# The first pair of a feed-forward as seven products instead of eight, and a new head of fourteen products

## The chip, the cores and the metric

The kernel runs on one core of a Trainium2 chip. The metric is the device time of one launch in microseconds (us). The kernel before takes 919.77 us, the median of three runs (919.72 to 920.04).

A core has five engines that run side by side, each with a queue that it works through in order: TensorE (PE) multiplies matrices from SBUF into PSUM, VectorE (DVE) and ScalarE (ACT) work element by element and may read and write both memories, GpSimd (POOL) does the same in SBUF alone, and SyncE (SP) issues DMA transfers. An instruction that waits for a semaphore holds up all that stands behind it on its own engine.

## The reference, cut to what matters

```python
x = x + 0.5 * rms_norm(swiglu_ffn(rms_norm(x, norm_pre[l, 0]), ffn1_w_in[l], ffn1_w_out[l]), norm_post[l, 0])
mixed = token_mixer(rms_norm(x, norm_pre[l, 1]), ...)
x = x + rms_norm(mixed, norm_post[l, 1])
x = x + 0.5 * rms_norm(swiglu_ffn(rms_norm(x, norm_pre[l, 2]), ffn2_w_in[l], ffn2_w_out[l]), norm_post[l, 2])

def swiglu_ffn(x, w_in, w_out):
    gate, up = jnp.split(x @ w_in, 2, axis=-1)
    return (jax.nn.silu(gate) * up) @ w_out
```

There are 512 tokens of width 1024, a feed-forward width of 2816, all in float32, and one layer. Each of the two feed-forwards computes gate and up (two products of 512 by 1024 with 1024 by 2816), a product of the two, and a last product back to width 1024. The change touches the first feed-forward's gate and up alone.

## The kernel before, in words

**Precision.** Each float32 operand is split in two fp32r parts, a high part (a copy that rounds) and a low part (what the copy left out). One product takes three matrix passes: high by high, high by low, low by high. For a weight tile the high part is an ACT cast of 128x1024 (line 294) and the low part a DVE subtraction of the same size (line 296), both in `split`.

**Pairs and products.** The 22 columns of 128 of gate and up are taken in 11 pairs, 0 to 10. Of a pair, gate and up and the two halves of the 1024 rows give four weight tiles of 512 KB: a (gate, upper rows), b (up, upper rows), c (gate, lower rows), d (up, lower rows). The tokens come in two halves of 256. Done plainly, a pair takes eight products of a weight tile with a block of the activations; `ffn_in` does a pair with seven, in the manner of Strassen and Winograd, from sums of weight tiles (line 310) and sums of activation blocks (`sums`, line 391). The products of a pair are called p1 to p7. p1 and p2 use the plain tiles a and c with the plain blocks of the first token half; p3 uses the plain tile d, and the four others use sums of weight tiles, or sums of activations, or both. A product (`prod`, line 604) is 24 matmuls of 128x256: 16 that read the weight tile's high part, then 8 that read its low part.

**The start.** The kernel begins with the first feed-forward, and there the sums of activations are not ready. So `HEADS` does pair 0 of the first feed-forward plainly, with eight products: c1 to c4 for the first token half, and e1 to e4 for the second, which use the same four weight tiles again (`held` keeps them in SBUF). Between these stand p1 and p2 of the pairs 1 and 2. That makes twelve products. While they run, `start` (line 736) writes out by hand in what order ACT, DVE and PE are given the rest: the norm of the token rows 2 and 3 (`norm`), their transposes, and the sums of activations, in five steps for each of the two rows (`to_s` begins a row's generator, and each `step(g2)` or `step(g3)` takes one step more). Every piece of work is issued where it stands in this text, and each engine's queue holds it in that order.

**The weight buffer.** The split weight tiles lie in one SBUF tile `w` with four places. `lie` (line 259) takes the first free place in the order of `free`; a place is given back when the product that reads it is issued (`drop`); and where no place at all is held, `split` sets the order anew: `if not self.slot and it.key[0] != "mix": self.free = deque(FREE2 if it.key[0] == "f2" else FREE)`, with `FREE = (2, 3, 0, 1)`. `full_split` splits one tile; `feed` splits tiles until four places are held. The first tiles go to three places of their own (`stay`), so three of pair 0's four tiles lie in these, and the fourth lies in place 2 of `w` from c2 until e2.

**Loads.** Weight tiles are loaded by SP into two rings, three buffers `raw` and five `raw2`, and a load waits until its buffer's last reader is done. The loads of the start are issued from the first us on, with those of x between them.

**The sums of weight tiles.** At the start POOL makes eight of them (pairs 1 and 2, four each; line 310, `late` is false); later DVE makes them. Each sum overwrites a raw tile, so it waits until that tile's last split is done, and the next split of the sum waits for POOL.

**After the head.** `ffn_in` runs the rest of `ORDER`, four tiles ahead (`feed`). For the pairs before `FILLED` the parts of a pair are added with DVE in SBUF; from there on more is gathered in PSUM. The second feed-forward has had its own head, `HEADS2`: p1 and p2 of seven pairs, fourteen products in all, none of which needs a sum of any kind; the tiles of the five pairs in `ONCE` are loaded for that alone and once more later.

## Time and profile before

| | |
|---|---|
| time, median of 3 runs | 919.77 us |
| time of the profiled execution | 920.66 us |
| its span (first to last instruction) | 918.9 us |
| mean granted TensorE clock over the span | 0.998 |
| DVE busy, ACT busy, POOL busy | 84%, 57%, 21% of the span |
| weight tiles of the two feed-forwards' first matrices loaded | 98, of 512 KB |

The profiled execution's time is 1.8 us over its span, for what lies around the first and last instruction. The rows that follow give for a group of instructions the line, the engine, the operation, what it writes and reads, the shape and type, the number of them, then the busy time and the mean in ns of one. A row of the timeline gives the start and the length of a run of like instructions in us, and in brackets the idle time of the engine before it and what ended that. The matmuls of one run overlap: one lasts 277 ns from its issue to its end, but they are issued every 114 to 118 ns.

### The profile page before, as it was taken

How to read it: one execution, taken by the hardware profiler on the slowest of the kernel's cores; microseconds unless marked ns; L12 is line 12 of the kernel's file. 1: busy time of each engine (PE TensorE's matmuls, PEld its weight loads, DVE VectorE, ACT ScalarE, POOL GpSimd, SP SyncE). 2: the span in 40 equal slices, each digit the busy share in tenths (PEclk: the TensorE clock that was granted, in tenths of full speed). 3: DMA queues.
4: the chain of work that ended last, by engine and by line, in shares of the span. 5: the costliest groups of instructions: out<-in, count | busy, mean ns of one | idle time of the engine just before them, and what ended most of it. 6: DMA issues, size and time to landing. Idle time of an engine off the chain costs nothing.

```text
span 918.9 us, 18150 instructions
## 1 busy us (share of the span) xinstructions
PE 910.2 (99%) x7332; PEld 877.3 (95%) x7332; DVE 768.1 (84%) x1007; ACT 524.2 (57%) x753; POOL 190.6 (21%) x267
## 2 busy tenths in 40 slices
PE   9999999999999999999999999999999999999997
PEld 8999999999999999998888887899999999999997
DVE  6899988889888877799877655699899989998886
ACT  7645555547666467957634345594454545757661
POOL 2531112121111047842330310313000000010002
PEclk9999999999999999999999999999999999999999
DMA  9355879775897825699852125252354445378542
GB/s 308 84 168 131 188 186 213 188 160 139 217 286 233 247 57 140 136 204 231 186 93 79 37 92 176 81 180 74 111 161 139 138 118 160 96 229 256 170 145 93
DMA packets 123384, 145.42 MB, mean 158 GB/s; under 512 B 12066, under 2 KB 96034, under 8 KB 123300
## 3 DMA queue, kind: packets, MB, share of 16 engines
q1 hardware_dynamic: 107332, 129.05, 46.3%
q0 software_dynamic: 15680, 14.69, 11.9%
q8 instruction: 57, 0.93, 0.4%
q10 hardware_dynamic: 288, 0.52, 0.2%
q14 instruction: 27, 0.22, 0.1%
HBM read 142.14 MB, written 31.46 MB: 189 GB/s over the span
## 4 chain that ended last, share of the span: by engine, by line
PE 57%; DVE 3%; ACT 2%; DMA 1%; issue 1%; SPq 0%; DVEq 0%; POOLq 0%; POOL 0%; ACTq 0%
PE ps L619 23%; PE ps L1012 8%; PE ps L549 5%; PE ps L1004 4%; PE ps L198 4%; PE ps L200 4%; PE ps L199 4%; PE ps L560 1%; PE ps L364 1%; DMA f2sums<-in_ffn_w_out_dram 1%; PE ps L1756 0%; PE ps L1451 0%; PE ps L1729 0%; DVE w L296 0%; DVE sT L1457 0%
## 5 line engine op out<-in xcount | busy, mean ns | idle before, releaser
L294 ACT CAST w<-raw 128x1024 fp32r<-128x1024 f32 x246 | 251.0, 1027 | 189.3 <-PE ps L619 89.4
L296 DVE TENSOR_TENSOR w<-raw,w 128x1024 fp32r<-128x1024 f32 x246 | 299.8, 1222 | 30.2 <-ACT w L294 28.8
L619 PE MATMUL ps<-xq,w 128*128 128x256 f32 x2016 | 237.4, 277 | 0.0
L619 PEld LDWEIGHTS ps<-xq,w 128*128 128x128 f32 x2016 | 233.2, 188 | 0.1
L619 PE MATMUL ps<-sq,w 128*128 128x256 f32 x1512 | 178.2, 277 | 0.0
L619 PEld LDWEIGHTS ps<-sq,w 128*128 128x128 f32 x1512 | 174.8, 188 | 0.0
L310 DVE TENSOR_TENSOR raw<-raw,raw 128x1024 f32<-128x1024 f32 x72 | 89.7, 1251 | 6.3 <-DMA raw<-in_ffn_w_in_dram 4.9
L1012 PE MATMUL ps<-w,hs 128*128 128x256 f32 x672 | 80.9, 276 | 0.0
L1004 PE MATMUL ps<-w,hs 128*128 128x256 f32 x672 | 79.2, 276 | 0.0
L1012 PEld LDWEIGHTS ps<-w,hs 128*128 128x128 f32 x672 | 78.3, 188 | 0.0
L1004 PEld LDWEIGHTS ps<-w,hs 128*128 128x128 f32 x672 | 77.5, 188 | 0.0
L198 PE MATMUL ps<-w,xq 128*128 128x512 f32 x176 | 71.6, 408 | 0.2 <-DVE sT L1457 0.2
L199 PE MATMUL ps<-w,xq 128*128 128x512 f32 x176 | 68.6, 391 | 0.0
L200 PE MATMUL ps<-w,xq 128*128 128x512 f32 x176 | 68.6, 391 | 0.0
L944 POOL DMA_DIRECT2D f2sums<-in_ffn_w_out_dram x15 | 20.1, 1484 | 175.2 <-DMA f2sums<-in_ffn_w_out_dram 174.9
L549 PE MATMUL ps<-xq,w 128*128 128x256 f32 x480 | 55.7, 277 | 0.0
L549 PEld LDWEIGHTS ps<-xq,w 128*128 128x128 f32 x480 | 54.9, 188 | 0.5 <-issue 0.5
L884 ACT CAST hs<-hf 128x1024 fp32r<-128x1024 f32 x32 | 33.7, 1053 | 28.0 <-PE ps L1012 20.3
L885 DVE TENSOR_TENSOR hs<-hf,hs 128x1024 fp32r<-128x1024 f32 x32 | 39.1, 1222 | 9.0 <-ACT hs L884 8.4
L944 POOL DMA_DIRECT2D f1sums<-f1sums x26 | 21.5, 828 | 110.0 <-DMA f1sums<-in_ffn_w_out_dram 57.9
L944 POOL DMA_DIRECT2D f2sums<-f2sums x30 | 26.1, 897 | 84.0 <-DMA f2sums<-in_ffn_w_out_dram 40.2
L310 POOL TENSOR_TENSOR raw<-raw,raw 128x1024 f32<-128x1024 f32 x12 | 32.6, 2721 | 40.9 <-DVE w L296 40.7
(279 smaller groups left out, 1248.0 us busy)
## 6 DMA issues: line engine op xcount, KB each, us to landing
raw<-in_ffn_w_in_dram SPq DMA_DIRECT2D x98, 512.0 KB, 4.7
raw<-in_ffn_w_out_dram SPq DMA_DIRECT2D x44, 512.0 KB, 4.9
raw<-in_w_mix_in_dram SPq DMA_DIRECT2D x28, 512.0 KB, 4.7
raw<-f2sums SPq DMA_DIRECT2D x15, 512.0 KB, 4.6
raw<-f1sums SPq DMA_DIRECT2D x13, 512.0 KB, 6.2
raw<-in_w_mix_out_dram SPq DMA_DIRECT2D x8, 512.0 KB, 3.9
f2sums<-in_ffn_w_out_dram SPq DMA_DIRECT2D x30, 128.0 KB, 6.0
f2sums<-in_ffn_w_out_dram SPq DMA_DIRECT2D x15, 256.0 KB, 6.0
```

The lines of the kernel that those rows point to most:

```text
L198: mm(ps, sh, mh, start=start, stop=False, **kw)
L199: mm(ps, sh, ml, start=False, stop=False, **kw)
L200: mm(ps, sl, mh, start=False, stop=stop, **kw)
L294: nc.scalar.copy(hi, raw)
L296: self.low = nc.vector.tensor_tensor(lo, raw, hi.bitcast(F32), op=ALU.subtract)
L310: added = (nc.vector if late else nc.gpsimd).tensor_tensor(o, o, c, op=ALU.add)
L549: mm(ps[:, u0:u1], w[:, a, k, :], self.xop(k, b, u0, u1), start=k + n + m == 0, stop=k == ND - 1 and n == 2, skip_group_check=True,)
L619: self.nc.tensor.matmul(ps[:, c], wb[b][:, k, v], left[d][:, k, :], start=first and a + n + k == 0, stop=n == 2 and k == KH - 1, skip_grou ...
L885: self.nc.vector.tensor_tensor(lo, src, hi.bitcast(F32), op=ALU.subtract)
L944: nc.gpsimd.dma_start(to[:, a:b], v, accum_op=ALU.add)
L1004: mm(out, a[kk][:, i * P : (i + 1) * P], w[:, b, kk, QUARTER * v : QUARTER * (v + 1)], start=begin and c == kk == n == 0, stop=kk == 1 and ...
L1012: mm(ps[:, QUARTER * c : QUARTER * (c + 1)], A[a][:, c], B[b], start=begin and c == n == 0, stop=n == 2, skip_group_check=True,)
```

## The change

The first feed-forward now does what the second did. Pair 0 is one more pair of seven products; the plain products c1 to e4 are gone, with the places that held their tiles. `HEADS` and `ORDER` are what `HEADS2` and `ORDER2` were, for both feed-forwards: the head is fourteen products, p1 and p2 of the pairs 3, 5, 7, 8, 6, 1 and 0, of which ten tiles (pairs 3, 5, 7, 8, 6) are loaded again later. The pairs follow as 0, 1, 2, 3, 4, 5, 9, 6, 7, 8, 10, `FILLED` is 2 for both, and POOL makes the eight sums of pairs 0 and 1. `start` is rewritten for the new head: p1's result is copied to SBUF with ACT before p2 adds to the same bank (line 616 of the change), and the places of the steps of the sums of activations are others. One product of 24 matmuls falls away.

The core of the diff:

```diff
-HEADS = [("c1", 0), ("c3", 0), ("c2", 0), ("c4", 0), ("p1", 1), ("e1", 0), ("e3", 0)]
-HEADS += [("e2", 0), ("p1", 2), ("p2", 1), ("e4", 0), ("p2", 2)]
...
-HEADS2, ORDER2 = (
+POOLED = {"f1": 2, "f2": 1}
+FILLED, ONCE, GATED = 2, (3, 5, 7, 8, 6), (1, 9, 6, 7)
 SEQ = (0, 1, 2, 3, 4, 5, 9, 6, 7, 8, 10)
+HEADS, ORDER = (
     [("p" + c[0], int(c[1])) for c in cs.split()]
     for cs in ("13 15 17 23 25 18 27 28 16 11 26 10 21 20", "50 51 60 61 70 30 40 71 31 12")
 )
...
+        alone = (7, 8) if name == "f2" else range(len(once))
+        own = {pt: [load(pt[1], place[pt[0]], None if n in alone else name, n)] for n, pt in enumerate(once)}
...
-                        nc.scalar.activation(L.col(), L.nhalf[:, :1], AF.Exp)
+                        nc.scalar.activation(L.col(), L.nhalf[:, :1], AF.Silu)
```

and in `start`, behind the first splits, as it now reads:

```python
        head, done = deque(HEADS), deque()

        def prod():
            self.lag()
            p, t = head.popleft()
            self.prod(p, t, False)
            done.append(lambda: self.after(p, t))

        after = lambda: done.popleft()()
        prod()
        root(2)
        self.full_split()
        prod()
        after()
        for h in range(2):
            nc.scalar.copy(gpre[:, v[h]], gain[h])
        self.full_split()
        norm(2)
        prod()
        step(q[0][1], q[1][1])
        step(q[0][1], q[1][1])
        self.full_split()
        step(q[0][0])
        after()
        self.to_s(2, xn[2])
        prod()
        root(3)
        after()
        self.full_split()
        norm(3)
        step(q[0][1], q[1][0], q[1][1])
        prod()
        after()
        self.full_split()
        self.to_s(3, xn[3])
        g2, g3 = self.gs
        prod()
        after()
        self.full_split()
        step(g2)
        prod()
        after()
        self.full_split()
        step(g3)
        for g in (g2, g3, g2, g3, g2, g3):
            prod()
            after()
            self.feed()
            step(g)
```

The head's products are called H1 to H14 below, in the order of `HEADS`: H1 to H3 are p1 of the pairs 3, 5, 7; H4 and H5 p2 of 3 and 5; H6 p1 of 8; H7 and H8 p2 of 7 and 8; H9 p1 of 6; H10 p1 of 1; H11 p2 of 6; H12 p1 of 0; H13 and H14 p2 of 1 and 0. In the rows, `raw_125`, `raw_30_210` and `raw_35_245` are the loaded tiles of H7, H8 and H9, `raw_37_278`, `raw_279` and `raw_398` those of H10, H11 and H12, and `raw_53_475` that of H13; `ps_320`, `ps_325` and `ps_400`, `ps_405` are the PSUM banks of the token rows 2 and 3, in which their sums are made; `sq_116` and `xq_76` are two of the blocks of activation sums. A semaphore's name tells which engine or queue is waited for.

**First place: the middle of the head.** ACT's queue in the kernel before, from the first tile of pair 2 (its p1, the ninth product) on:

```order
L294 CAST w<-raw_212 128x1024 [waits DMAHW2_49]
L398 CAST sq_116<-ps_336 128x4x128 [waits DVE_49,PE_49,Activation_49]
L646 COPY hf_113<-ps_386 128x2x256
L398 CAST sq_116<-ps_376 128x4x128 [waits DVE_49,PE_49]
L294 CAST w<-raw_11_124 128x1024 [waits DMAHW1_49]
L398 CAST xq_76<-ps_331 128x4x128 [waits DVE_49,PE_49,Activation_49]
L294 CAST w<-raw_212 128x1024 [waits PE_49,Pool_49]
```

and in the change, from the cast of H7's tile on:

```order
L278 CAST w<-raw_125 128x1024 [waits DMAHW0_49,DVE_49,PE_49]
L382 CAST sq_116<-ps_325 128x4x128 [waits DVE_49]
L616 COPY hf_113<-ps_413 128x2x256 [waits PE_49]
L278 CAST w<-raw_30_210 128x1024 [waits DMAHW1_49,PE_49,Activation_49]
L382 CAST sq_116<-ps_405 128x4x128 [waits DVE_49]
L618 ACTIVATE hf_113<-ps_285 128x2x256 [waits PE_49]
L278 CAST w<-raw_35_245 128x1024 [waits DMAHW2_49,PE_49,Activation_49]
```

Before, the casts of plain tiles (the first and the fifth row; the last is of a sum) wait for their load alone, since the places that they write are free. In the change each cast waits for PE as well (`PE_49`: the sixteenth matmul of the product before, the last that reads the high part of the same place), and between two of them stand a cast of a sum of activations, which waits for DVE, and a copy or Silu of a product's result.

DVE's queue at the same place, in the kernel before:

```order
L296 TENSOR_TENSOR w<-raw_212,w 128x1024 [waits DMAHW2_49,Activation_49]
L638 TENSOR_TENSOR hf_113<-ps_249,hf_113 128x2x256
L397 TENSOR_TENSOR ps_331<-ps_336,hf_113 128x512 [waits DVE_49]
L397 TENSOR_TENSOR ps_336<-ps_336,hf_113 128x512
L397 TENSOR_TENSOR sq_116<-ps_336,sq_116 128x4x128 [waits PE_49,Activation_49]
L397 TENSOR_TENSOR ps_371<-ps_376,hf_113 128x512 [waits DVE_49]
L397 TENSOR_TENSOR ps_376<-ps_376,hf_113 128x512
L397 TENSOR_TENSOR sq_116<-ps_376,sq_116 128x4x128 [waits Activation_49]
L296 TENSOR_TENSOR w<-raw_11_124,w 128x1024 [waits DMAHW1_49,Activation_49]
```

and in the change:

```order
L280 TENSOR_TENSOR w<-raw_125,w 128x1024 [waits DMAHW0_49,PE_49,Activation_49]
L381 TENSOR_TENSOR ps_320<-ps_325,hf_113 128x512
L381 TENSOR_TENSOR ps_325<-ps_325,hf_113 128x512
L381 TENSOR_TENSOR sq_116<-ps_325,sq_116 128x4x128 [waits Activation_49]
L280 TENSOR_TENSOR w<-raw_30_210,w 128x1024 [waits DVE_49,DMAHW1_49,PE_49,Activation_49]
L381 TENSOR_TENSOR ps_400<-ps_405,hf_113 128x512
L381 TENSOR_TENSOR ps_405<-ps_405,hf_113 128x512
L381 TENSOR_TENSOR sq_116<-ps_405,sq_116 128x4x128 [waits Activation_49]
L280 TENSOR_TENSOR w<-raw_35_245,w 128x1024 [waits DVE_49,DMAHW2_49,PE_49,Activation_49]
```

Each low part in the change waits for PE, which is the last matmul of the product before; the two subtractions that the next cast of ACT needs stand behind it. The place in `w` is the same one for the tiles of H3 to H9: in `start` each `full_split` comes after the `prod` that gave back the only place held, so the order of places is set anew and place 2 is taken each time. The first tiles that go to other places are those of H10 to H12, from the first `feed`.

**Second place: behind H9's tile.** ACT's queue in the change, from the cast of H10's tile to the copy of H9's result (`ps_524`), the bank to which H11 then adds:

```order
L278 CAST w<-raw_37_278 128x1024 [waits DMAHW3_49]
L278 CAST w<-raw_279 128x1024 [waits DMAHW4_49]
L278 CAST w<-raw_398 128x1024 [waits DMAHW4_49]
L382 CAST xq_76<-ps_320 128x4x128 [waits DVE_49]
L618 ACTIVATE hf_113<-ps_413 128x2x256 [waits PE_49]
L278 CAST w<-raw_53_475 128x1024 [waits DMAHW0_49,PE_49,Activation_49]
L382 CAST xq_76<-ps_400 128x4x128 [waits DVE_49]
L616 COPY hf_113<-ps_524 128x2x256 [waits PE_49]
```

DVE's queue at the same place:

```order
L280 TENSOR_TENSOR w<-raw_37_278,w 128x1024 [waits DMAHW3_49,Activation_49]
L280 TENSOR_TENSOR w<-raw_279,w 128x1024 [waits DMAHW4_49,Activation_49]
L280 TENSOR_TENSOR w<-raw_398,w 128x1024 [waits DMAHW4_49,Activation_49]
L381 TENSOR_TENSOR ps_325<-hf_113,ps_320 128x512
L381 TENSOR_TENSOR xq_76<-ps_320,xq_76 128x4x128 [waits Activation_49]
L280 TENSOR_TENSOR w<-raw_53_475,w 128x1024 [waits DVE_49,DMAHW0_49,PE_49,Activation_49]
L381 TENSOR_TENSOR ps_405<-hf_113,ps_400 128x512
L381 TENSOR_TENSOR xq_76<-ps_400,xq_76 128x4x128 [waits Activation_49]
```

H11's first matmul waits for the ACT row that copies `ps_524` (it is `ps_524<-xq_75,w 128x256 [waits Activation_49]` in PE's queue). Before that copy, ACT has casts of activation sums that wait for the subtractions which stand behind three low parts on DVE. In the kernel before, the one such copy in the rows above (`hf_113<-ps_386`, of p1 of pair 1) stands ahead of the cast of the tile that p2 of pair 1 reads.

More of the change, by code (lines that the diff above doesn't have):

```diff
@@ L401, in sums @@
         a22 = self.hf[:, 10 + i, :].rearrange("p (c t) -> p c t", c=KH)
[L402 to L405 removed]
+        s1, s2, s3, s4 = (self.left[n] for n in ("p5", "p6", "p7", "p3"))
+        two = self.left["p4"]
         hi(two, p1)
         nc.scalar.copy(a22, p1)
[L408 to L409 removed]
         self.lowed = lo(two, p1)
@@ L855, in ffn_in @@
                     nc.gpsimd.drain()
-            with self.behind(*(self.c22 if p in ("p3", "p5") and self.second else ())):
+            with self.behind(*(self.c22 if p in ("p3", "p5") else ())):
                 self.feed()
@@ L1226, in load @@
         def load(t, r, group=None, once=None):
-            even = (SEQ.index(t) if second else t) % 2 == 0 and r != "c" if once is None else once in (5, 6, 9)
+            even = SEQ.index(t) % 2 == 0 and r != "c" if once is None else once in (5, 6, 9)
             ring = ("raw", 3) if even else ("raw2", 5)
```

174 lines of the change are left out of this document (57 added, 117 removed).

## The prediction

> **What bounds the kernel now.** First the page's sums by engine, then the two groups of L619, its product loop.
>
> ```profile
> span 918.9 us, 18150 instructions
> PE 910.2 (99%) x7332; PEld 877.3 (95%) x7332; DVE 768.1 (84%) x1007; ACT 524.2 (57%) x753; POOL 190.6 (21%) x267
> L619 PE MATMUL ps<-xq,w 128*128 128x256 f32 x2016 | 237.4, 277 | 0.0
> L619 PE MATMUL ps<-sq,w 128*128 128x256 f32 x1512 | 178.2, 277 | 0.0
> ```
>
> PE is busy 99% of the span, and no idle time stands before its products. A busy PE alone says little, so I looked next at who makes PE wait, from 8 us to 240 us of the span (most of the first feed-forward).
>
> ```profile
> PE ps L364 <- DVE xn L754: 0.2, 1, 0.2
> PE ps L619 <- ACT xq L384: 0.2, 1, 0.2
> ```
>
> These two waits, 0.4 us together, are all of them. So PE bounds this stretch, and whatever makes it wait in the change is added to the time in full: nothing behind has slack to give it back. The timeline of PE gives the price of a product.
>
> ```profile
> 10.63 5.82 PE L619 MATMUL ps<-xq,sq 128*128 128x256 f32 x48 [0.19 <-ACT xq L384]
> ...
> 31.92 8.38 PE L619 MATMUL ps<-xq,w 128*128 128x256 f32 x72
> ...
> 51.37 14.30 PE L619 MATMUL ps<-sq,w 128*128 128x256 f32 x120
> ```
>
> Three products take 8.38 us and five 14.30, so one of 24 matmuls takes **2.8 us**. The first starts at 10.63, and so does the change's: the queues up to there are the same but for one activation table.
>
> **What falls away.** One product: -2.8 us. Everything behind the first feed-forward has the same instructions in the same order.
>
> **What is added, and hidden.** Ten more loads of 512 KB, three more casts, three low parts and four sums. The windows show the room.
>
> ```profile
> 10.63:51.40 40.77, 40.77 (x353) 40.52 (x354) 34.23 (x41) 28.31 (x45) 17.34 (x14) 1.00 0.53 154
> 65.50:240.00 174.50, 174.50 (x1536) 174.50 (x1535) 156.88 (x173) 95.74 (x121) 29.92 (x32) 1.00 0.73 177
> ```
>
> The columns after the length are busy us of PE, PEld, DVE, ACT, POOL, then clock, share of the DMA engines and GB/s. In the head, DMA is half free; the tiles of H1 to H8 are issued where the loads of before stood in SP's queue. The tile of H12 stands behind the small parameter loads there, and one of these is long:
>
> ```profile
> 22.77 5.44 SPq L1297 DMA_DIRECT2D prm<-in_conv_b_dram  x1
> ...
> raw<-in_ffn_w_in_dram SPq DMA_DIRECT2D x98, 512.0 KB, 4.7
> ```
>
> SP comes to H12's load near 31.5 us; even at twice the 4.7 us in which the page has such a load land, it is there before ACT asks for it (41.8, below). In the stretch behind the head, DMA has a quarter free for some 2 MB more, and the second feed-forward runs this very order of pairs with no wait of PE's. I take 0; were that cover gone (DVE has 10% left there), a late tile or sum would cost up to some 5 us, which I keep for the upper end.
>
> **What is added, and not hidden: one place for seven tiles.** H3 to H9 all use place 2 of `w`. So the next tile's cast waits for the sixteenth matmul before, and its low part for the last. The durations come from these groups (8 to 75 us, shapes apart).
>
> ```profile
> L294 ACT CAST w<-raw 128x1024 fp32r<-128x1024 f32 x18 | 18.7, 1055 | 12.2 <-DVE raw L310 8.3 <-POOL raw L310 2.3 <-DMA raw<-in_ffn_w_in_dram 0.9
> L398 ACT CAST sq<-ps 128x512 fp32r<-128x512 f32 x6 | 3.4, 593 | 6.7 <-DVE ps L397 5.8 <-PE ps L619 0.9
> L731 ACT ACTIVATE hf<-xs 128x1024 f32<-128x1024 f32 x2 | 2.1, 1059 | 0.0
> L388 ACT COPY hf<-ps 128x512 f32<-128x512 f32 x4 | 2.0, 582 | 0.0
> L296 DVE TENSOR_TENSOR sq<-raw,sq 128x1024 fp32r<-128x1024 f32 x3 | 3.7, 1217 | 0.0
> L397 DVE TENSOR_TENSOR ps<-ps,hf 128x512 f32<-128x512 f32 x4 | 2.6, 686 | 0.0
> ```
>
> A cast takes 1.05 us, a copy or a cast of a sum 0.59, a low part 1.22, a subtraction in PSUM 0.69. Instructions that follow each other overlap by 0.1 (the timeline has the four copies of L388 in 2.02), so in a queue I count 0.95, 0.48, 1.13 and 0.6. A semaphore costs about 0.1.
>
> Bare handoff: sixteen matmuls end 1.9 us into a product, 2.05 with what a matmul takes beyond its issue; cast 1.05, semaphore 0.1: the next product starts 3.2 us after this one, not 2.8. That is **0.4 us** at least, unless the eight transposes of a token row (0.85 us) stand between.
>
> Now the queues, from the first product on.
> - H4: the second half of row 2's transposes waits for a copy on ACT that stands behind H4's cast: +0.5. H4 starts at 20.55.
> - H5: after that copy, ACT has four copies and casts and one Square ahead of H5's cast (4 x 0.48 + 1.06): the cast runs from 22.85 to 23.9 where PE would be ready at 23.4: +0.6.
> - H6: row 3's transposes hide it: 0. H7: the bare handoff, +0.45; it starts at 30.95.
> - H8 and H9: DVE may do H7's low part only when H6 has ended and the cast is done, at 30.9. Behind it stand two subtractions, then ACT's cast of a sum, a copy, and H8's cast: 1.13 + 0.6 + 0.69 + 0.1 + 0.48 + 0.48 + 1.05 + 0.1 = 4.6 us from start to start, against 2.8. H9 repeats it. **+1.8 each**; H8 starts at 35.5, H9 at 40.1, its cast done at 40.0.
> - H11: it waits for the copy of H9's result. From 40.0, DVE has four low parts (3 x 1.13 + 1.22 = 4.6), a subtraction (0.6); ACT a cast, a Silu and H13's cast (0.1 + 0.48 + 0.48 + 1.05); DVE H13's low part and a subtraction (1.13 + 0.69), ACT a cast and the copy (0.48 + 0.59), with three more semaphores 0.3. That is 10.5 us: H11 at 50.5. PE has H9 and H10 until 45.7: **+4.8**.
>
> **POOL's adds on top of it.** POOL's first sums (pairs 1 and 0) are released by the low parts of H10 and H12, in this same stretch. What they do to DVE shows in the timeline.
>
> ```profile
> 29.35 4.88 POOL L310 TENSOR_TENSOR raw<-raw,raw 128x1024 f32<-128x1024 f32 x2 [1.16 <-DVE w L296]
> 29.79 1.28 DVE L397 TENSOR_TENSOR ps<-ps,hf 128x512 f32<-128x512 f32 x2
> ...
> 40.42 2.41 POOL L310 TENSOR_TENSOR raw<-raw,raw 128x1024 f32<-128x1024 f32 x1 [6.18 <-DVE w L296]
> ...
> 41.30 2.61 DVE L296 TENSOR_TENSOR w<-raw,w 128x1024 fp32r<-128x1024 f32 x1 [0.36 <-ACT w L294]
> ...
> 51.08 6.79 POOL L310 TENSOR_TENSOR raw<-raw,raw 128x1024 f32<-128x1024 f32 x2 [1.16 <-DVE w L296]
> ...
> 52.78 2.83 DVE L296 TENSOR_TENSOR w<-raw,w 128x1024 fp32r<-128x1024 f32 x1
> ```
>
> A low part that starts while POOL adds ends 1.1 us after POOL does (43.91 against 42.83); it waits the add out. Subtractions that read PSUM are not held up (1.28 for two). In the change, POOL's first add waits for H10's low part, finds DVE at H11's, and runs 2.26 us from 43.5; H12's low part then ends at 46.9 instead of 44.65. POOL's second add starts with that end and its third at 49.45; H13's low part is ready at 49.6, 0.15 us too late, and ends at 52.9. That adds 2.25 and 2.2: H11 starts at 54.9, **9.2 instead of 4.8**. The last 0.15 is a near thing: if DVE comes first, 2.2 less. Without any such block, 4.8 stands; I take 9.2, since every low part of the rows that met an add was held.
>
> The Trainium skill, SBUF — State Buffer, "SBUF: two separate sides", says that a DVE instruction with two SBUF inputs and a GpSimd one that reads SBUF exclude each other for a whole instruction, whoever starts first; the rows agree (1.22 becomes 2.61), and by it the sum stays.
>
> **The clock.** PE then stands still from 45.7 to 54.9.
>
> ```profile
> 912.40:915.90 3.50, 0.00 (x0) 0.00 (x0) 2.50 (x5) 0.47 (x2) 0.81 (x2) 1.00 0.45 170
> 915.90:918.90 3.00, 0.00 (x0) 0.00 (x0) 0.00 (x0) 0.00 (x0) 0.00 (x0) 0.51 0.41 151
> 1.23 3.65 PE L194 MATMUL ps<-ones 128*128 128x128 f32 x16 [1.23 <-POOL ones L172]
> ...
> 7.02 0.61 PE L194 MATMUL ps<-ones 128*128 128x128 f32 x4
> ```
>
> At the end of the span the granted clock falls to half 3.5 us after the last matmul, and the first sixteen matmuls take 3.65 us where later four take 0.61 (0.11 each from issue to issue). So a pause of 9.2 us is followed by some 3.4 us at half speed: 1.6 us lost, between 0 (if the clock holds) and 3.
>
> The Trainium skill, TensorE: Matmul & The Clock Gate, "Why this matters for your kernels", warns of PE pauses over about 3 us in the middle of a kernel; the trace agrees at its end, where 3.5 us brought the clock to 0.51. By that rule the pauses of 1.8 us cost nothing more.
>
> **The sum.** 0.5 + 0.6 + 0.45 + 1.8 + 1.8 + 9.2 + 1.6 - 2.8 = +13.1 us. From H12 on, tiles and sums are ahead of PE again, as the pause gave the others time. The profiled execution took 920.66 us, 0.9 over the median: 933.8 for one like it, and **933** against the median.
>
> **Rivals.**
> - *No block by POOL, or DVE first* (H11 waits 4.8 to 7.0): 15.15 - 4.4 = +8.7, or +10.9: 928.5 to 930.7. The rows speak against the first; 0.15 us decides the second. Chance 0.25.
> - *More than this:* the same, and late tiles or sums in the new body of the first feed-forward, up to 5 us: 935 to 938. For it: DVE is busy 90% there and DMA 73%. Against: the second feed-forward's same order has no wait. 0.12.
> - *Handoffs alone:* ACT and DVE keep up, and only the one place costs: H5, H7, H8, H9, 4 x 0.4 = 1.6, and H4's 0.5, less 2.8: 919.1, within 0.2%. It needs the sums of activations not to stand ahead of the casts, which the order denies. 0.06.
> - *Faster:* the head runs with no wait, as the second feed-forward's does: 919.8 - 2.8 = **917.0**. The point from which it decides: all waits of the head together below 0.9 us, and one bare handoff is 0.4. It is also the case if the casts did not truly wait for the place (a wait on PE that is met early). 0.06.
>
> **How the numbers follow.** Forecast 0.51 (931 to 935), the rivals 0.25, 0.12, 0.06, 0.06. The range goes from 926, just under the first rival, to 936.5: it leaves out the last two and half of the second. A measurement of this kernel can tell about 0.2% (1.8 us) from no change. Faster 0.06, same 0.06, slower 0.88.
>
> **What would show it.** In the profile after: PE's groups of L595 with idle time, ended by ACT `w` L278 (about 5 us in all) and once by ACT `hf` L616, 5 to 9 us in one piece near 46 us; product starts 4.6 us apart before that; DVE's low parts of 2.4 us or more beside POOL's adds; a mean granted clock below 0.998 and a stretch of half clock near 55 us. Wrong would be: a PE that is busy from 10.6 us on without a gap, or gaps whose releaser is a DMA, or gaps behind 70 us.

## The result, and the profile after

The changed kernel takes 942.5 us (median of four runs, 941.2 to 947.8) where the kernel before takes 919.9 in the same session: a ratio of 1.0252, with a 95% interval of 1.0232 to 1.0272. It is slower, as forecast, but by 22.6 us and not by 13, and outside the range of 926 to 936.5. Below, the head is H1 to H14, and the body is the rest of the first feed-forward's gate and up.

The page's first lines and the two groups of its product loop (now line 595), to be laid beside those of before:

```profile
span 939.5 us, 18138 instructions
PE 913.7 (97%) x7308; PEld 879.1 (94%) x7308; DVE 775.0 (82%) x1011; ACT 526.9 (56%) x758; POOL 193.0 (21%) x267
L595 PE MATMUL ps<-xq,w 128*128 128x256 f32 x2016 | 242.2, 279 | 12.3 <-ACT hf L616 8.7
L595 PE MATMUL ps<-sq,w 128*128 128x256 f32 x1584 | 186.7, 277 | 3.4 <-DVE ps L613 3.4
```

Before, no idle time stood ahead of the products. Now 15.7 us do. The list of PE's waits between 8 and 260 us (what it waited for, us in all, times, longest):

```profile
PE ps L595 <- ACT hf L616: 8.7, 1, 8.7
PE ps L595 <- ACT w L278: 3.6, 4, 1.5
PE ps L595 <- DVE ps L613: 3.4, 3, 1.7
```

The first two rows are the head: one pause at a copy of a p1 result, four at casts of weight tiles. The third is new ground: three pauses behind 100 us, in the body of the first feed-forward, where the prediction had none. PE's timeline shows the head's pauses in place:

```profile
31.77 3.10 PE L595 MATMUL ps<-xq,w 128*128 128x256 f32 x24 [0.21 <-ACT w L278]
36.28 3.00 PE L595 MATMUL ps<-xq,w 128*128 128x256 f32 x24 [1.42 <-ACT w L278]
40.80 5.83 PE L595 MATMUL ps<-xq,w 128*128 128x256 f32 x48 [1.51 <-ACT w L278]
55.30 14.91 PE L595 MATMUL ps<-xq,w 128*128 128x256 f32 x103 [8.67 <-ACT hf L616]
```

These are H7, H8, H9 with H10, and H11 with what follows it. The windows around the long pause (length, then busy us of PE, PEld, DVE, ACT, POOL, granted clock, DMA share, GB/s):

```profile
46.63:51.26 4.63, 0.00 (x0) 0.00 (x0) 3.24 (x4) 2.02 (x3) 3.50 (x2) 1.00 0.14 48
51.26:55.30 4.04, 0.00 (x1) 0.00 (x1) 3.39 (x3) 1.13 (x3) 1.19 (x1) 0.50 0.00 0
55.30:61.50 6.20, 6.20 (x29) 6.20 (x30) 3.21 (x5) 3.99 (x6) 0.00 (x0) 0.50 0.00 0
61.50:70.00 8.50, 8.50 (x76) 8.50 (x76) 6.93 (x8) 5.46 (x8) 5.48 (x3) 1.00 0.01 2
```

The clock stands at half from 51.26 to 61.50, so PE works 6.2 us at half speed behind the pause: 3.1 us lost.

**Where the time went.** To see where the difference arises, take each product's start, counted from the first product's, and subtract the same of before. The change has one product fewer, so its k-th product is set beside the k+1-st of before, and H1 reads -2.9. A number that grows to the right is time lost between two columns. "End of gate and up" is the end of the 76th of the 77 products, behind which the first matmuls of the out-projection (the feed-forward's product back to width 1024) stand. The differences, for the change and for the experiments below, in us (worked out from the starts of the matmuls in the traces, each of one profiled execution; the last column is the median of all):

| kernel | H11 | first product of the body | 46th product | end of gate and up | median time |
|---|---|---|---|---|---|
| changed kernel | 11.7 | 14.3 | 16.4 | 18.3 | 942.5 |
| e1_places | 10.1 | 11.4 | 19.5 | 24.3 | 942.1 |
| e2_two | 5.1 | 6.4 | 14.2 | 18.2 | 940.9 |
| e14_warm | 11.7 | 11.4 | 21.8 | 22.3 | 945.5 |
| e6_dve | 10.8 | 13.1 | 15.4 | 19.7 | 940.3 |
| e7_two_dve | 6.5 | 6.3 | 16.7 | 19.8 | 941.5 |
| e8_ahead | 4.9 | 7.1 | 16.9 | 16.9 | 940.5 |
| e9_quiet | 11.7 | 13.6 | 15.6 | 15.5 | 936.9 |
| e10_quiet_ahead | 5.0 | 6.8 | 10.4 | 10.5 | 932.3 |
| e11_early | 4.9 | 6.1 | 6.8 | 8.9 | 933.8 |
| e12_cast_first | 1.3 | 1.9 | 5.2 | 7.4 | 928.7 |
| e13_quiet_dve | 10.7 | 12.1 | 12.3 | 12.2 | 933.6 |
| e15_copy_first | 0.8 | 2.0 | 1.2 | 5.3 | 929.4 |
| e16_floor | 0.8 | 2.0 | 1.2 | 1.1 | 922.8 |

For the changed kernel: 14.3 us in the head, 4.0 in the body, and by the spans (939.5 against 918.9) 20.6 in all. Of the 2.3 that are left, 0.8 is the first product's start (11.41 instead of 10.63), and 1.5 comes behind gate and up. The rest of the 22.6 lies between single executions: the profiled one took 941.23, the median is 942.5. (The row of e1_places is of an execution of 947.1 us, the slowest of its four.)

### The profile page after: what moved, and what is told of

It reads as the page before. It is cut to its first block, busy times and chain, and to the rows that moved or that the text cites. A ratio compares the mean times of both kernels' runs of the same rounds, so it can differ in the third digit from the quotient of the medians.

```text
span 939.5 us, 18138 instructions
## 1 busy us (share of the span) xinstructions
PE 913.7 (97%) x7308; PEld 879.1 (94%) x7308; DVE 775.0 (82%) x1011; ACT 526.9 (56%) x758; POOL 193.0 (21%) x267
## 4 chain that ended last, share of the span: by engine, by line
PE 56%; DVE 3%; ACT 2%; issue 1%; DVEq 0%; POOLq 0%; POOL 0%; ACTq 0%
PE ps L595 22%; PE ps L983 8%; PE ps L529 5%; PE ps L975 4%; PE ps L182 4%; PE ps L183 4%; PE ps L184 4%; PE ps L540 1%; PE ps L348 1%; DVE w L280 0%; DVE qk L1571 0%; PE ps L1708 0%; PE ps L1403 0%; PE ps L1681 0%; DVE sT L1409 0%
## 5 line engine op out<-in xcount | busy, mean ns | idle before, releaser
L278 ACT CAST w<-raw 128x1024 fp32r<-128x1024 f32 x250 | 254.4, 1028 | 194.4 <-PE ps L595 105.8
L280 DVE TENSOR_TENSOR w<-raw,w 128x1024 fp32r<-128x1024 f32 x250 | 308.4, 1239 | 39.1 <-ACT w L278 35.6
L595 PE MATMUL ps<-xq,w 128*128 128x256 f32 x2016 | 242.2, 279 | 12.3 <-ACT hf L616 8.7
L595 PEld LDWEIGHTS ps<-xq,w 128*128 128x128 f32 x2016 | 236.9, 190 | 13.3 <-ACT hf L616 8.9
L595 PE MATMUL ps<-sq,w 128*128 128x256 f32 x1584 | 186.7, 277 | 3.4 <-DVE ps L613 3.4
L595 PEld LDWEIGHTS ps<-sq,w 128*128 128x128 f32 x1584 | 182.9, 188 | 3.9 <-issue 1.9
L294 DVE TENSOR_TENSOR raw<-raw,raw 128x1024 f32<-128x1024 f32 x76 | 94.1, 1247 | 17.3 <-DMA raw<-in_ffn_w_in_dram 13.5
L529 PE MATMUL ps<-xq,w 128*128 128x256 f32 x480 | 55.7, 277 | 0.0
L529 PEld LDWEIGHTS ps<-xq,w 128*128 128x128 f32 x480 | 54.9, 188 | 0.5 <-issue 0.5
```

Of the source, the lines that this page charges most:

```text
L278: nc.scalar.copy(hi, raw)
L280: self.low = nc.vector.tensor_tensor(lo, raw, hi.bitcast(F32), op=ALU.subtract)
L294: added = (nc.vector if late else nc.gpsimd).tensor_tensor(o, o, c, op=ALU.add)
L529: mm(ps[:, u0:u1], w[:, a, k, :], self.xop(k, b, u0, u1), start=k + n + m == 0, stop=k == ND - 1 and n == 2, skip_group_check=True,)
L595: self.nc.tensor.matmul(ps[:, c], wb[b][:, k, v], left[d][:, k, :], start=first and a + n + k == 0, stop=n == 2 and k == KH - 1, skip_grou ...
```

## The experiments

### Which wait makes the head's pauses

**e1_places** lets the places of `w` take turns in the first feed-forward.

```diff
-            if not self.slot and it.key[0] != "mix":
+            if not self.slot and it.key[0] != "mix" and (it.key[0] == "f2" or not self.free):
```

> The changed kernel, but the weight places rotate in the head of the first feed-forward instead of all of H3 to H9 using place 2. Queue theory (the waits come from weight casts that stand on ACT behind casts of sums, and these behind DVE's subtractions and four low parts): the chain stays; H8 and H9 still wait about 1.4 us each and H11 6 to 9 us; 1 to 3 us faster than the changed kernel, about 940. Place theory (the one place makes the waits): the waits of H5, H7, H8, H9 go and most of H11's, no half clock behind it; 10 to 16 us faster, 927 to 932.

```profile
34.04 3.00 PE L595 MATMUL ps<-xq,w 128*128 128x256 f32 x24 [1.17 <-ACT w L278]
38.56 5.84 PE L595 MATMUL ps<-xq,w 128*128 128x256 f32 x48 [1.51 <-ACT w L278]
53.06 7.20 PE L595 MATMUL ps<-xq,w 128*128 128x256 f32 x47 [8.66 <-ACT hf L616]
```

942.1 us, ratio 1.0232 (1.0181 to 1.0284). In PE's timeline the pauses of H8, H9 and H11 are there as before (1.42, 1.51 and 8.67); only H7's wait of 0.21 and a little of H4's, H5's and H8's are gone. The one place is not what makes the long ones: the place theory falls, and what the one place costs ahead of H11 is 1.5 us in all (11.7 to 10.1 in the table). In the body three waits of 2.2 to 3.0 us, each with half clock behind it, took more than that back.

**e2_two** casts and splits two tiles instead of four ahead of the sums in the last loop of `start`.

```diff
             after()
-            self.feed()
+            self.feed(2)
             step(g)
```

> The changed kernel, but two weight tiles instead of four are cast and split ahead of the sums in the last part of the head. Queue theory (H11 waits because the sums of H9 stand on DVE behind four low parts): the pause ahead of H11 falls from 8.7 us to about 2.5, PE's clock does not fall to half, so 6 us and 3 us come back: about 933. Place theory: nothing changes, 940 to 943.

```profile
35.37 2.99 PE L595 MATMUL ps<-xq,w 128*128 128x256 f32 x24 [1.50 <-ACT w L278]
39.88 5.84 PE L595 MATMUL ps<-xq,w 128*128 128x256 f32 x48 [1.53 <-ACT w L278]
47.91 18.27 PE L595 MATMUL ps<-xq,w 128*128 128x256 f32 x144 [2.19 <-ACT hf L616]
```

The pause is 2.19 instead of 8.67, as the queue theory says. But the time is 940.9, ratio 1.0239 (1.0209 to 1.0269), not 933: the table shows PE 7.9 us earlier at the body's first product (6.4 against 14.3) and level again at the end of gate and up (18.2 against 18.3). New pauses of 1.2 and 1.7 us near 87 and 90, one of 2.27 near 184, and half clock behind both places took it back. (The clock still fell behind the 2.19, but for 3.4 us and not for 10.2.) The head was understood; the body was not.

### Do POOL's adds hold DVE's low parts

**e3_adds** moved POOL's first three sums behind H13's split in the program.

```diff
...
+            if it.key[0] == "f1" and self.done in (9, 11):
+                self.kept_adds, adds = getattr(self, "kept_adds", ()) + adds, ()
+            elif it.key[0] == "f1" and self.done == 12:
+                adds = self.kept_adds + adds
...
```

> The changed kernel, but POOL's first three sums of weight tiles are issued only behind the low part of H13, out of the stretch in which H11 waits. If POOL's adds hold DVE's low parts (the prediction's step): low parts of H12 and H13 take 1.2 us instead of 2.4 or more, and the pause ahead of H11 falls from 8.7 us to 4.3 to 5; the half clock behind it may stay or go. If they don't: the pause stays at 8 to 9 us. The sums come later, which the body may pay for with up to 3 us.

Its pause was 8.63 and its time 944.5, ratio 1.0260 (1.0239 to 1.0280). It tested nothing: POOL has an empty queue there and waits for its data alone, so a later place in the program moved them by less than 0.1 us: counted from the first product, the first add starts at 31.7 us here and at 31.8 in the changed kernel. **e5_adds** adds to the same edit a real dependence, a one-column copy on POOL that reads the low part of H13 and stands ahead of the sums:

```diff
...
+                nc.gpsimd.tensor_copy(seen, lo[:, KH - 1, 2 * P - 1 :].bitcast(F32))
...
```

> The changed kernel with POOL's first three sums held back by a small copy on POOL that reads the low part of H13 (e3_adds moved them in the program only: they wait for nothing but their data, and ran at the same moments). If POOL's adds hold DVE's low parts: the four low parts take 4.6 us in a row and not 6.83, H13's takes 1.2 and not 3.24, and the pause ahead of H11 falls from 8.7 us to 4.3 to 5. If the adds hold nothing: 8.2 to 8.7 again. The sums then come up to 6 us later, so the refill of the weight tiles and the waits of the body get no better, rather worse.

The low parts on DVE and the adds on POOL, in the timelines of the changed kernel:

```profile
40.77 6.83 DVE L280 TENSOR_TENSOR w<-raw,w 128x1024 fp32r<-128x1024 f32 x4 [0.74 <-ACT w L278]
50.29 3.24 DVE L280 TENSOR_TENSOR w<-raw,w 128x1024 fp32r<-128x1024 f32 x1 [0.74 <-ACT w L278]
43.22 3.31 POOL L294 TENSOR_TENSOR raw<-raw,raw 128x1024 f32<-128x1024 f32 x1 [18.89 <-DVE w L280]
47.69 4.77 POOL L294 TENSOR_TENSOR raw<-raw,raw 128x1024 f32<-128x1024 f32 x2 [1.16 <-DVE w L280]
```

and DVE's and PE's in e5_adds:

```profile
39.87 4.63 DVE L280 TENSOR_TENSOR w<-raw,w 128x1024 fp32r<-128x1024 f32 x4 [0.74 <-ACT w L278]
47.19 1.23 DVE L280 TENSOR_TENSOR w<-raw,w 128x1024 fp32r<-128x1024 f32 x1 [0.73 <-ACT w L278]
50.18 10.09 PE L602 MATMUL ps<-xq,w 128*128 128x256 f32 x62 [4.46 <-ACT hf L623]
```

Four low parts take 4.63 us without an add beside them and 6.83 with one; H13's takes 1.23 and not 3.24; and the pause ahead of H11 is 4.46 instead of 8.67. So 4.2 us of it are POOL's lock, and the rest the queue chain. The kernel's time, 954.0 (ratio 1.0369, 1.0348 to 1.0390), does not tell of this: its matmuls are issued more slowly all through (116.1 ns apart between 640 and 760 us, where the changed kernel has 113.5). Why is not shown. The edit adds a tile of one column, which may shift the addresses of the tiles behind it; that was not tried.

### What the half clock costs

**e4_warm** gives PE 70 matmuls of 128x128 into an unused bank behind H10.

```diff
+            if len(head) == 4:
+                keep = self.bank["p1", 0] = self.ps()
+                for _ in range(70):
+                    nc.tensor.matmul(keep[:, :P], self.ident, self.ident, start=True, stop=True)
```

> The changed kernel with 70 matmuls of 128x128 into an unused PSUM bank behind H10, so that PE works through the pause ahead of H11. If the half clock comes from the pause: no half clock between 51 and 62 us, H11 to H13 run at 0.11 us a matmul from the start, and some 3 us come back (the prediction had 1.6): about 938. If it comes from something else: the clock record still falls to half for some 10 us, and the time stays. H11 starts at the same time in both.

Each of them ran as two of 0.113 us: 140 records from 45.61 to 61.40 us, so H11 came some 7 us late and the kernel took 949.9, ratio 1.0318 (1.0277 to 1.0359). The clock stayed full there, which is all that this run tells. **e14_warm** has 37 of them.

> e4_warm with 37 matmuls instead of 70: each leaves two records of 0.113 us, so they fill 8.4 us and end about when H11 may start. If the half clock is the pause's: no half clock near 50 to 60 us, H11 to H14 at 0.113 us a matmul, H11's start as in the changed kernel, and some 3 us come back up to the first product of the body (1.6 by the prediction's term); the body may give part of it back.

```profile
46.29 8.42 PE L803 MATMUL ps<-ident 128*128 128x128 f32 x74
55.12 15.08 PE L595 MATMUL ps<-xq,w 128*128 128x256 f32 x130 [0.41 <-ACT hf L616]
...
54.72:62.00 7.28, 6.88 (x60) 6.88 (x61) 6.20 (x8) 6.23 (x10) 2.29 (x1) 1.00 0.00 0
```

H11 starts where it did (55.12 here, 55.30 in the changed kernel), with the clock at 1.00: 60 matmuls in 7.3 us, where the changed kernel did 29 in 6.2. By the table the body's first product comes at 11.4 instead of 14.3. So the half clock behind the pause cost 2.9 us, where the prediction had 1.6. Again the body took back more than that: pauses of 2.44 and 3.57 us near 102 and 136, each followed by half clock, and 945.5 us in the end (ratio 1.0260, 1.0229 to 1.0295).

### What the body is short of

The changed kernel's DVE waits for weight tiles to land between 60 and 250 us; that of before had no such wait there.

```profile
DVE raw L294 <- DMA raw<-in_ffn_w_in_dram: 9.6, 5, 2.8
```

**e6_dve** gives pair 1's sums to DVE, which leaves POOL four sums instead of eight.

```diff
-POOLED = {"f1": 2, "f2": 1}
+POOLED = {"f1": 1, "f2": 1}
```

> The changed kernel with the four sums of pair 1 on DVE instead of POOL in the first feed-forward, as the second has them. Sum theory (the body's waits come from POOL's eight sums, of which three run from 69.3 to 78.4 us and hold SP, which issues no load from 44.7 to 71.8 us and the next at 78.5): the refill is issued 4 to 7 us earlier, the body's waits of 3.4 us fall below 1, the pause ahead of H11 becomes 7 to 8.7; 936 to 939. Traffic theory (the body's waits come from the f1sums transfers or from DMA being busy): the waits of the body stay at 3 us or more, 940 to 943.

940.3 us, ratio 1.0214 (1.0169 to 1.0259). The first of the body's waits, near 104 us, went; the two later ones grew from 0.6 and 1.7 to 2.1 and 2.5, as the traffic theory has it. So POOL's sums made the first wait, and not the others. SP's gap without a load still ends at 70.4 us (71.8 in the changed kernel), but the load behind it is issued at 72.8 and not at 78.5. **e7_two_dve** joins it to e2_two:

> e2_two and e6_dve together: two low parts ahead of the sums, and the sums of pair 1 on DVE. e2_two brought the pause ahead of H11 from 8.7 to 2.2 us and gave it back in the body (waits of 5.5 us, two stretches of half clock). Sum theory: with POOL's eight sums cut to four, the body's waits stay below 1.5 us and the clock stays full: 927 to 931. If the body is short of something else (DMA or DVE as a whole), the gain of the head is given back again: 937 to 941.

941.5 us, ratio 1.0228 (1.0208 to 1.0249): 8 us gained at the body's first product (6.3), all given back by its end (19.8), most of it in one wait of 4.3 us near 131. **e8_ahead** adds the turning places and one more tile ahead from H8 on:

```diff
...
         self.full_split()
+        self.full_split()
         step(g2)
...
```

> e7_two_dve, with the weight places in turn also in the head of the first feed-forward, and one more tile cast and split ahead, from H8 on: each cast of a weight tile then stands on ACT ahead of the casts of sums instead of behind them. Queue theory: the waits of H8 (1.4), H9 (1.5) and H11 go, all waits of the head together below 1.5 us, and with no wait in the body 918 to 922, the change's 2.8 us nearly paid for. Against it (ACT and DVE have too little time for what the head adds): waits of 3 us or more stay in the head, 924 to 930.

940.5 us, ratio 1.0225 (1.0196 to 1.0253): a miss in both parts. H9's wait went, but H8's (1.36) and 5.06 of H11's stayed, for a reason that its timelines show. DVE:

```profile
35.10 1.23 DVE L280 TENSOR_TENSOR w<-raw,w 128x1024 fp32r<-128x1024 f32 x1 [0.74 <-ACT w L278]
36.24 1.29 DVE L381 TENSOR_TENSOR ps<-ps,hf 128x512 f32<-128x512 f32 x2
```

and ACT:

```profile
34.01 1.06 ACT L278 CAST w<-raw 128x1024 fp32r<-128x1024 f32 x1
37.57 0.59 ACT L382 CAST sq<-ps 128x512 fp32r<-128x512 f32 x1 [2.50 <-DVE ps L381]
38.05 0.60 ACT L618 ACTIVATE hf<-ps 128x512 f32<-128x512 f32 x1
38.54 1.05 ACT L278 CAST w<-raw 128x1024 fp32r<-128x1024 f32 x1
```

DVE's low part waits for ACT's cast of the tile, its subtractions stand behind the low part, ACT's cast of the sum waits for these, and the next tile's cast stands behind that: 4.5 us from cast to cast (34.01 to 38.54), however many tiles are ahead. And in the body waits of 6.2 us in all, 4.7 of them near 130, took back what was gained.

The changed kernel, e2_two, e6_dve, e7_two_dve and e8_ahead reach the body's first product up to 8 us apart (6.3 to 14.3), yet end gate and up between 16.9 and 19.8 us late. Whatever the head gives is taken back in the body, which waits for weight tiles. In the trace of e8_ahead, DVE stands idle for 6.5 us until 123.9; the load that it waits for was issued at 113.9 and landed at 123.8, after 9.9 us where the median one of that kernel takes 4.6. Around it lie the sums' transfers: sums of blocks of the out-projection's weights (f1sums) are made in device memory, where SP copies one block (here two such sums, at 107 to 111) and POOL then issues DMAs that add another to it (here at 112.7 and 114.9). **e9_quiet** leaves these adds by DMA out of the changed kernel:

```diff
-                nc.gpsimd.dma_start(to[:, a:b], v, accum_op=ALU.add)
+                if f == "f2":
+                    nc.gpsimd.dma_start(to[:, a:b], v, accum_op=ALU.add)
```

> The changed kernel without the adds by DMA of the f1sums transfers (POOL's three a sum are left out, half of their bytes; the copies on SP stay, and the first feed-forward's quarter sums are wrong by that). Traffic theory (in the first feed-forward's body the loads of weight tiles land late because the sums' transfers share the DMA engines, and DVE's sums wait for them): DVE's waits for DMA between 60 and 250 us fall from 9.6 us to below 3, PE's waits of 3.4 us in the body to below 1, 936 to 939. Buffer theory (the loads are late because they are issued late, whatever else DMA does): both stay, 940 to 943.

936.9 us, ratio 1.0180 (1.0165 to 1.0196): the time is what the traffic theory gave, but the waits fell less than it said. DVE's wait for landing tiles is 4.8 instead of 9.6 (expected: below 3), and of PE's three waits behind 60 us the two later ones are gone; the first, POOL's, stays, at 1.7 us (expected: below 1):

```profile
PE ps L595 <- DVE ps L613: 1.7, 1, 1.7
```

**e13_quiet_dve** joins this to e6_dve.

> e9_quiet and e6_dve together: the changed kernel without the f1sums adds by DMA (half of their bytes; the quarter sums are wrong by that), and with the sums of pair 1 on DVE. e6_dve removed the body's first wait (near 104 us) and left the later ones, e9_quiet removed the later ones and left the first. If POOL's sums and the sums' transfers are all of it: no wait of PE above 0.5 us between 60 and 240 us, 934 to 936. If there is a third cause: 1 us or more of waits stays.

```profile
PE ps L595 <- ACT w L278: 0.3, 1, 0.3
```

This row is all of PE's waits between 60 and 260 us that the view lists. By the table the body adds 0.1 us (12.1 to 12.2) where the changed kernel's adds 4.0. So, with the head's long pause still in place, the two causes together are the whole of the changed kernel's loss in the body: POOL's sums, behind which SP's loads wait, and the adds by DMA of the sums' transfers. 933.6 us, ratio 1.0141 (1.0125 to 1.0157). DVE still waits 8.8 us for landing tiles in this trace, and PE does not, so the length of DVE's waits does not tell whether PE waits.

**e10_quiet_ahead** is e8_ahead without the adds by DMA.

> e8_ahead with the same adds by DMA left out. Traffic theory: the body's waits of 6.2 us and the half clock behind them (1.7 us) fall below 1 us, and what e8_ahead saved in the head is no longer given back: 929 to 932. Buffer theory: no change from e8_ahead, 938 to 941.

932.3 us, ratio 1.0141 (1.0113 to 1.0169), at the upper edge of what the traffic theory gave: of what e8_ahead gained in the head, 3.7 us instead of 9.8 are given back (6.8 to 10.5 in the table). The waits of the body fell from 6.2 to 2.3 us, and not below 1: behind a faster head the body is still short of something that the two causes, cut down in this way, leave.

### Versions that compute everything

**e11_early** is e8_ahead with the transfers of the sums begun nine products earlier and at a slower pace.

```diff
-            if n > 14 and n % EVERY == 0 and not self.second:
+            if n > 1 and n % 6 == 0 and not self.second:
```

> e8_ahead, but the f1sums transfers begin some ten products earlier and one every six products instead of five, since DMA is busy only 36% between 80 and 110 us and 80 to 90% behind. Complete computation. Traffic theory: the body's waits of 6.2 us fall to 1 to 4, 932 to 937. Buffer theory: no change, 938 to 941.

933.8 us, ratio 1.0148 (1.0125 to 1.0171); one wait of 1.9 us is left in the body. With the same transfers in all, the body lost 9.8 us in e8_ahead and 2.8 here (6.1 to 8.9): so when they run matters, and not only how many they are. **e12_cast_first** also issues the tile's cast ahead of the step of sums, and its low part behind it:

```diff
+        def cast_first(g):
+            split = self.split()
+            next(split)
+            step(g)
+            next(split)
...
-        self.full_split()
-        step(g3)
+        cast_first(g3)
...
-            self.feed(2)
-            step(g)
+            cast_first(g)
```

(The last lines are set against e8_ahead's.)

> e11_early, with each weight tile's cast issued on ACT ahead of the step of activation sums beside it, and its low part on DVE behind that step, so that ACT and DVE no longer wait for each other in turn (in e8_ahead they took 4.5 us from product to product). Queue theory: the waits of H8 (1.4) and H11 (5.1) fall below 2 us together, no half clock near 50 us, 6 to 8 us faster than e11_early: 925 to 930. If DVE has too little time there: waits of 3 us or more stay.

928.7 us, ratio 1.0101 (1.0084 to 1.0118). The time is within what was expected, with 5.1 us gained on e11_early and not 6 to 8: H8's wait is still 1.36 and H11's is 1.42 instead of 5.05 (expected: below 2 together), and no half clock is left. ACT's casts of tiles there start at 33.86, 36.42, 39.50 and 43.83 us, 2.6 to 4.3 us apart. In the body waits of 3.8 us are left. **e15_copy_first** puts the copies of p1 ahead of the casts of sums, one more tile ahead, and all sums on DVE; what else follows a product in the head is issued one product later than before. One line of the edit, set against e12_cast_first's:

```diff
...
             next(split)
+            copy_now()
             step(g)
...
```

> e12_cast_first, with the copies of p1 products (for which H8 and H11 wait) issued on ACT ahead of the casts of activation sums, one more tile ahead, and all sums of weight tiles of the first feed-forward on DVE, so that POOL locks nothing there. Complete computation. If queues and locks are what is left in the head: its waits fall from 4.3 us to below 1.5, 923 to 926. If DVE as a whole is short: waits of 3 us stay, 927 to 931. The change's own gain is 2.8, so nothing below 917 is possible.

929.4 us, ratio 1.0094 (1.0068 to 1.0120): no better than e12_cast_first, and in the range that was given for a DVE short of time (no run tests whether it is). H8's wait is gone, but H11's is 2.55, with half clock behind it; in the body one wait of 2.4 us is left, with half clock behind it too, and one of 1.4 us in the out-projection. **e16_floor** is the same without the adds by DMA.

> e15_copy_first without the f1sums adds by DMA (the quarter sums are wrong by that): what the change could give at most if those transfers cost its loads nothing. With no waits left in head and body 917 to 920; if the supply of weight tiles stays short without them, 921 to 925.

922.8 us, ratio 1.0028 (1.0015 to 1.0042). No wait of PE is left in the body, and it loses nothing (2.0 to 1.1 in the table); what is left is the head's waits, of which H11's of 2.55 us is the largest. So with this head the change is not faster than the kernel before even where half of the transfers' bytes are left out. Of the versions that compute everything e12_cast_first and e15_copy_first are the best, equal within their intervals, some 9 us slower than before.

## Why the prediction was wrong

**Right: the head, step by step.** Counted from the first product, the prediction put H5 at 13.4, H7 at 20.3, H8 at 24.9, H9 at 29.5 and H11 at 44.3 us. The trace has 13.4, 20.4, 24.9, 29.4 and 43.9. The queue chain is what makes these waits (e1_places, e2_two), and not the one place that the prediction's heading names: with the places in turn, H8, H9 and H11 wait nearly as before (1.17, 1.51 and 8.66). The chain's parts are as costed: POOL's lock was put at 4.45 us and e5_adds shows 4.2; the chain without it at 4.8, and e5_adds has 4.46. Two small things in its working do not hold: the first rival's "15.15 - 4.4" should start from 13.15, from which its results (+8.7, 928.5) are right; and no row stood for the 0.1 us of a semaphore. In the trace of before, ACT starts 0.04 us after the DVE instruction that it waits for and DVE 0.03 after ACT's, in the median.

**The rule on the lock held.** What the Trainium skill, SBUF — State Buffer, "SBUF: two separate sides", says of DVE and GpSimd excluding each other for a whole instruction is borne out: 6.83 us for four low parts beside an add, 4.63 without.

**Mis-sized: "some 3.4 us at half speed: 1.6 us lost".** The half clock lasted 6.2 us of PE's work and cost 3.1 by the clock record, 2.9 by e14_warm. With it the head comes to 14.3 and not 13.1, though H11 itself comes 0.4 us earlier than forecast.

**Wrong: "I take 0" for the body.** This is the step that failed: the prediction named gaps behind 70 us as a sign of being wrong, and there are three, of 3.4 us. The body costs 4.0 us, and with it goes part of the 1.5 behind it (one wait of 0.9 us in the out-projection, which e9_quiet doesn't have; the cause of the rest stays open). Against the 933.8 that the prediction gave for an execution like the profiled one, the 941.2 are 7.4 more, which is to within 0.1 the sum of 4.0 in the body, 1.5 behind it, 1.2 in the head and 0.8 at the first product. The argument was that DMA has a quarter free and that the second feed-forward runs this very order with no wait. Both were true and neither bore on it. The second feed-forward has this order without the sums' transfers and with half of POOL's sums (in the changed kernel's trace DMA is busy 0.44 of the time there, between 625 and 805 us); and the free quarter was a mean. In the changed kernel the mean is lower still than before (DMA busy 0.68 of the time between 60 and 240 us, 0.74 before), and the tiles still come late, since what is moved when has changed:

```profile
63.75 0.59 SPq L938 DMA_DIRECT2D f1sums<-in_ffn_w_out_dram  x1
...
50.00:80.00 30.00, 30.00 (x259) 30.00 (x259) 29.82 (x36) 17.32 (x20) 9.04 (x4) 1.00 0.61 172
```

These are SP's timeline and a window of the kernel before; the changed kernel has these, and the row of SP's waits between 40 and 90 us:

```profile
113.13 0.60 SPq L909 DMA_DIRECT2D f1sums<-in_ffn_w_out_dram  x1
...
50.00:80.00 30.00, 24.70 (x191) 24.70 (x192) 24.50 (x22) 15.72 (x24) 16.29 (x7) 0.83 0.08 21
110.00:140.00 30.00, 29.36 (x257) 29.20 (x257) 27.32 (x29) 15.29 (x19) 6.96 (x7) 1.00 0.89 227
...
SPq L239 <- POOL raw L294: 32.4, 2, 26.1
```

SP issues no load between 44.7 and 71.8 us, because it waits for POOL's sums, DMA lies almost idle until 80 us, and the refill and the sums' transfers then fall together: 0.89 busy between 110 and 140 us. The kernel before has a gap without loads of weight tiles too, from 20.2 to 54.6 us, in which SP waits 23.3 us for a sum of POOL's; but it ends 17 us earlier, and the first transfers of sums follow at 63.75 and not at 113 us.

**The rival that was nearest.** "More than this", late tiles and sums in the new body, up to 5 us, was right in kind and size (4.0 in the body), but had a chance of 0.12, and the range ended in its middle. That PE's pause "gave the others time" held only for the kernel as it was: e2_two, e7_two_dve, e8_ahead and e14_warm took the pause or its clock away, and the body asked it back.

**Outside the sum.** The first product's later start (0.8) is no part of the change: in the profiles of the experiments it lies at 10.5 to 10.7 us where the clock first rises before 5.2 us (before: at 4.60), and at 11.2 to 11.6 where it rises behind 5.7 (the changed kernel: at 6.89).

## What to carry to other kernels

A stretch in which an engine is "free on average" is not free: ask when each transfer becomes issuable, what stands ahead of it in its queue, and how far ahead of its use it lands; the mean share of the DMA engines did not show it here. A wait that is taken away ahead of a stretch that is short of tiles can be given back inside it, so cure the last limit first, or measure the shift product by product to see where a gain goes. Where two in-order queues feed each other in turn, the order inside one round decides: the same work took 4.5 us a round with the low part ahead of the subtractions, and 2.6 to 4.3 with the cast issued first.

## What the runs showed of the hardware

**The clock falls by a grid in time, not by a pause's length.** Full and half clock begin and end in steps of 3.41 us. In e1_places a pause of 2.16 us brought half clock, in e7_two_dve one of 3.45 did not:

```profile
101.23:103.39 2.16, 0.00 (x2) 0.00 (x1) 2.16 (x4) 0.68 (x2) 0.00 (x0) 1.00 0.00 0
104.17:107.59 3.42, 3.42 (x19) 3.42 (x18) 3.42 (x5) 0.00 (x0) 0.00 (x0) 0.50 0.45 149
...
46.71:50.16 3.45, 0.00 (x0) 0.00 (x0) 2.34 (x3) 1.55 (x4) 0.00 (x0) 1.00 0.15 37
50.16:60.00 9.84, 9.84 (x85) 9.84 (x86) 9.10 (x10) 8.41 (x13) 5.67 (x2) 1.00 0.12 43
```

The first two rows are e1_places, the others e7_two_dve. Laid on the grid that the clock record's own steps give, the pause of 2.16 lies in one step (100.76 to 104.17), while that of 3.45 is parted into 1.71 and 1.74. Over the first feed-forward's gate and up in all the profiles, each of the 24 steps at full clock in which PE was idle for some 2 us or more (1.98 to 3.41) was followed by half clock, and none with 1.75 or less; at 1.9 it went both ways. The clock rose again behind each of the 25 steps at half clock with 0.4 us or less of idle, and behind none of the 16 with 0.6 or more: in the changed kernel the step from 54.67 to 58.09 had 0.63 us of idle at its start, and half clock stayed to 61.50. So a pause can cost more clock than the prediction's 1.6 us (3.1 in the changed kernel), and one of 2.16 us cost 1.7 more (24 matmuls in 4.60 us instead of 2.88). This differs from the rule that the prediction drew on (the Trainium skill, TensorE: Matmul & The Clock Gate, "Why this matters for your kernels", pauses over about 3 us); the measurement decides.

**A byte added by DMA takes more of the DMA engines' time than a byte copied.** The two DMA queues of the changed kernel between 60 and 240 us (packets, MB, share of 16 engines):

```profile
q1 hardware_dynamic: 24420, 26.88, 48.1%
q0 software_dynamic: 4753, 4.46, 19.7%
```

The second is POOL's adds: 4.4% of the engines' time for each MB, where SP's loads and copies take 1.8%; in the kernel before it is 4.3% and 1.9%. Leaving out these 4.5 of 31.6 MB (e9_quiet) brought the loads' median landing from 5.1 to 4.5 us.
